# A norm's scale taken from half a row: the first feed-forward of a decoder layer

## The chip, the cores and the metric

The kernel runs on one core of one Trainium2 chip. The metric is the device time of one execution in microseconds, as the median of several runs. The engines are TensorE (PE, matrix products and transposes), VectorE (DVE), ScalarE (ACT), GpSimd (POOL) and SyncE (SP), whose queue issues nearly all DMAs.

## The reference

One layer on 256 tokens of width 2048, all in float32: a SwiGLU feed-forward of inner width 5632 (half of it added to the residual), a mixer, a cross-attention, a second such feed-forward and a last norm. The change touches the first feed-forward:

```python
def rmsnorm(x, g):
    xf = x.astype(jnp.float32)
    y = xf * lax.rsqrt(jnp.mean(xf * xf, axis=-1, keepdims=True) + EPS)
    return (y * g.astype(jnp.float32)).astype(x.dtype)

def swiglu(x, w_gate, w_up, w_down):
    return (jax.nn.silu(x @ w_gate) * (x @ w_up)) @ w_down

h = h + 0.5 * swiglu(rmsnorm(h, g_ffn1[l]), w1_gate[l], w1_up[l], w1_down[l])
```

## The kernel before

Every product is a sum of three in a reduced format: a float32 matrix is split into a rounded high half and the low half that is left (`split`: ACT casts the high half, DVE subtracts it for the low one), and high x high, low x high and high x low are accumulated. So every weight tile `f1gw` of 128 x 2048 costs ACT one cast (`f1gwh`) and DVE one subtraction (`f1gwl`).

The gate and up products of the first feed-forward run as eleven *units*, each of eight *chunks* along the inner dimension; a chunk is one weight tile of 1 MB against one *pair*, the two 128-column blocks of the 256 tokens' rows turned so that the inner dimension lies on the partitions. A chunk of kind N or C is 24 products of 128 x 512 on PE. Kind S multiplies 2 x 2 blocks by a seven-product scheme, 21 products; it needs sums of weight blocks (`f1gt`, and their halves `f1gth` and `f1gtl`) and sums of the pair's blocks (`n1f`, with high and low halves `n1fh` and `n1fl`). From the third unit on the chunks are S and C in turn.

The first unit (unit 0) doesn't wait for the norm. It multiplies the unnormalized rows, loaded already turned from `xT` (`n0r`, halves `n0h` and `n0l`) and scaled by the gain alone, and takes in the row's factor at the gating. Meanwhile the norm is made: four blocks of 512 columns of `h` are loaded, ACT squares and sums each for both token blocks (`square_into`, tile `junk`, sums in `parts`), `rstd_of` makes the factor (DVE reduces to `ss` and scales to `ms`, POOL raises to the power -1/2, `rs`), and `normalized(j)` has ACT scale two pairs' worth of rows at a time (`n1s`). PE then turns them by four transposes per pair (tile `n`), ACT applies the gain (`n1r`), and the halves are split. Units 1 to 10 read these pairs, eight of them, through `have(n1, i)`. The first serves unit 1's chunk 0.

`prep1(i)` is called once the load of chunk i of unit 0 is written, and with 8 + i beside chunk i of unit 1. It says at which chunk a block is loaded, squared and normalized. What it normalizes is turned by a generator, `work`, which is advanced after every sixth product, so its steps come at set places in PE's order. PE's order is the order in which the code issues. The other engines' orders are set by the scheduler of the framework, and all engines take their instructions in that order.

At a unit's end `late` combines the seven sums (`seven_late`, with DVE), and `gated` applies SiLU (ACT) and multiplies (DVE, line 699 without a factor, line 701 with one):

```python
nc.scalar.activation(sg[1], sg[0], AF.Silu, scale=1.0 if r is None else r[:, tb:tb + 1])
if r is None:
    nc.vector.tensor_tensor(sg[1], up, sg[1], ALU.mult)
else:
    nc.vector.scalar_tensor_tensor(
        out=sg[1], in0=up, scalar=r[:, tb:tb + 1], in1=sg[1], op0=ALU.mult, op1=ALU.mult
    )
```

Units 1 to 10 of the first feed-forward pass no factor. The second feed-forward does: its rows are scaled by the norm of their left half, and `rstd_left` makes what is left to the full norm. Tiles of the first feed-forward's gate units begin with `f1g`, those of the second with `f2g`. Banks of PE's accumulator are called `f1gP...`, `f1gQ...` and `f1gR`.

## Time and profile before

| | us |
|---|---|
| median of 3 runs | 2035.32 (2033.4 to 2035.91) |
| the profiled execution | 2033.63 |
| its span | 2031.9 |
| PE busy | 2015.5 (99%) |
| DVE busy | 1853.6 (91%) |
| ACT busy | 1313.2 (65%) |
| POOL busy | 34.4 (2%) |

The span runs from the first to the last recorded instruction; the profiled execution's time is 1.73 us longer. A row of a timeline gives the start and the length in microseconds, the engine, the line of the kernel, the operation, the tile written and the tiles read, and in brackets how long the engine had been idle and what released it. A row of waits gives a sum in microseconds, a count and the longest. Matmuls overlap, so their lengths say less than the distance of their starts.

### The profile page before, as it was taken

What the parts mean: (1) busy time and instruction counts of PE and PEld (TensorE: products, weight loads), DVE (VectorE), ACT (ScalarE), POOL (GpSimd) and SP (SyncE); (2) the same over time, 40 slices, a digit from 0 to 9 for tenths busy, and PEclk for the clock granted to TensorE, in tenths of its full rate; (3) what the DMA queues carried; (4) which work ended last, traced back from release to release, by engine and by line L of the source; (5) the groups of instructions that cost most, each with busy time, mean ns of one, the idle gap of its engine ahead of it and who ended that gap; (6) DMA issues with size and microseconds to landing.
All of it is one profiled execution on the core that took longest, in us unless ns stands there. A gap on an engine that the chain in (4) does not pass through costs nothing.

```text
span 2031.9 us, 24271 instructions
## 1 busy us (share of the span) xinstructions
PE 2015.5 (99%) x9203; PEld 1668.8 (82%) x9203; DVE 1853.6 (91%) x1994; ACT 1313.2 (65%) x1460; POOL 34.4 (2%) x57
## 2 busy tenths in 40 slices
PE   9999999999999999999999999999999999999998
PEld 7788888888888888888888888888888888888886
DVE  6999999999999978989879987899999999999998
ACT  7765566567665766755566666676656666676664
POOL 0000000000000010200000000000000000000000
PEclk9999999999999999999999999999999999999999
DMA  8666666666556575544675544556566656665563
GB/s 312 197 206 225 215 218 205 236 209 220 196 191 219 177 252 178 202 166 166 208 227 182 198 160 145 187 187 224 197 239 215 215 205 231 214 219 206 187 228 125
DMA packets 115333, 415.83 MB, mean 205 GB/s; under 512 B 61824, under 2 KB 63888, under 8 KB 68112
## 3 DMA queue, kind: packets, MB, share of 16 engines
q1 hardware_dynamic: 112768, 407.14, 57.6%
q0 software_dynamic: 2016, 6.30, 1.0%
q8 instruction: 72, 1.18, 0.2%
q10 hardware_dynamic: 432, 0.84, 0.1%
q14 instruction: 45, 0.37, 0.1%
HBM read 398.52 MB, written 2.10 MB: 197 GB/s over the span
## 4 chain that ended last, share of the span: by engine, by line
PE 85%; DVE 9%; issue 3%; ACT 2%; DMA 2%; SPq 0%; POOL 0%; POOLq 0%; DVEq 0%; ACTq 0%
PE f1gQ L428 12%; PE f2gQ L428 12%; PE f2dQ L428 6%; PE f1dQ L428 6%; PE f1gP L428 5%; PE f2gP L428 4%; PE xqQ L428 3%; PE f2dP L428 3%; PE f1dP L428 3%; PE woQ L428 2%; PE xoQ L428 2%; PE f2dR L428 2%; PE f1dR L428 2%; DVE f1gwl L148 2%; PE vQ L428 2%
## 5 line engine op out<-in xcount | busy, mean ns | idle before, releaser
L148 DVE TENSOR_TENSOR f1gwl<-f1gw,f1gwh 128x1536 fp32r<-128x1536 f32 (+2 forms) x94 | 181.6, 1934 | 24.5 <-ACT f1gwh L147 23.8
L147 ACT CAST f2gwh<-f2gw 128x1536 fp32r<-128x1536 f32 (+1 forms) x88 | 150.5, 1712 | 66.4 <-PE f2gQ L428 44.9
L148 DVE TENSOR_TENSOR f2gwl<-f2gw,f2gwh 128x1536 fp32r<-128x1536 f32 (+1 forms) x88 | 179.1, 2036 | 8.0 <-ACT f2gwh L147 8.0
L147 ACT CAST f1gwh<-f1gw 128x1536 fp32r<-128x1536 f32 (+2 forms) x94 | 153.1, 1629 | 45.0 <-PE f1gQ L428 19.3
L147 ACT CAST f1gth<-f1gt 128x1024 fp32r<-128x1024 f32 x76 | 79.9, 1051 | 103.1 <-DVE f1gt L337 68.7
L147 ACT CAST f2gth<-f2gt 128x1024 fp32r<-128x1024 f32 x82 | 85.4, 1050 | 64.2 <-DVE f2gt L341 34.0
L428 PE MATMUL f2gQ<-f2gwh,n4fh 128*128 128x512 f32 x317 | 123.8, 390 | 0.6 <-DVE f2gv L587 0.6
L428 PE MATMUL f2gQ<-f2gwh,n4fl 128*128 128x512 f32 x317 | 123.4, 389 | 0.0
L428 PE MATMUL f1gQ<-f1gwh,n1fl 128*128 128x512 f32 x286 | 111.4, 390 | 1.7 <-DVE n1fl L148 1.7
L428 PE MATMUL f1gQ<-f1gwh,n1fh 128*128 128x512 f32 x286 | 111.6, 390 | 0.0
L147 ACT CAST f2dwh<-f2dw 128x2048 fp32r<-128x2048 f32 (+1 forms) x44 | 77.4, 1758 | 47.5 <-PE f2dQ L428 39.5
L147 ACT CAST f1dwh<-f1dw 128x2048 fp32r<-128x2048 f32 (+1 forms) x44 | 77.3, 1757 | 43.7 <-PE f1dQ L428 42.7
L148 DVE TENSOR_TENSOR f1dwl<-f1dw,f1dwh 128x2048 fp32r<-128x2048 f32 (+1 forms) x44 | 92.0, 2092 | 12.0 <-ACT f1dwh L147 11.8
L148 DVE TENSOR_TENSOR f2dwl<-f2dw,f2dwh 128x2048 fp32r<-128x2048 f32 (+1 forms) x44 | 92.0, 2091 | 11.2 <-ACT f2dwh L147 11.1
L148 DVE TENSOR_TENSOR f2gtl<-f2gt,f2gth 128x1024 fp32r<-128x1024 f32 x82 | 99.5, 1218 | 1.0
L428 PE MATMUL f2gQ<-f2gwl,n4fh 128*128 128x512 f32 x317 | 96.7, 389 | 0.0
L148 DVE TENSOR_TENSOR f1gtl<-f1gt,f1gth 128x1024 fp32r<-128x1024 f32 x76 | 92.2, 1216 | 0.5
L428 PE MATMUL f1gQ<-f1gwl,n1fh 128*128 128x512 f32 x286 | 86.9, 389 | 0.0
L428 PEld LDWEIGHTS f2gQ<-f2gwh,n4fh 128*128 128x128 f32 x317 | 59.5, 188 | 13.8 <-DVE f2gv L587 1.6
L428 PEld LDWEIGHTS f2gQ<-f2gwh,n4fl 128*128 128x128 f32 x317 | 59.5, 188 | 12.2
L428 PEld LDWEIGHTS f2gQ<-f2gwl,n4fh 128*128 128x128 f32 x317 | 59.4, 188 | 12.3
L428 PE MATMUL f2gP<-f2gwh,n4fh 128*128 128x512 f32 x176 | 68.6, 390 | 0.0
(824 smaller groups left out, 6072.2 us busy)
## 6 DMA issues: line engine op xcount, KB each, us to landing
f2gw<-in_w_gu SPq DMA_DIRECT2D x88, 1024.0 KB, 4.9
f1gw<-in_w_gu SPq DMA_DIRECT2D x86, 1024.0 KB, 4.8
f1dw<-in_w_down SPq DMA_DIRECT2D x44, 1024.0 KB, 4.8
f2dw<-in_w_down SPq DMA_DIRECT2D x44, 1024.0 KB, 4.8
wow<-in_w_out SPq DMA_DIRECT2D x16, 1024.0 KB, 4.8
xqw<-in_w_xq SPq DMA_DIRECT2D x16, 1024.0 KB, 4.8
xow<-in_w_xo SPq DMA_DIRECT2D x16, 1024.0 KB, 4.8
qw<-in_w_in SPq DMA_DIRECT2D x8, 1024.0 KB, 4.8
```

The costliest lines, as they stand in the source:

```text
L147: nc.scalar.copy(hi, src)
L148: nc.vector.tensor_tensor(lo, src, hi.bitcast(F32), ALU.subtract)
L428: nc.tensor.matmul(self.banks[name], x, y, start=name not in self.begun, stop=self.left[name] == 0)
```

## The change

The factor for the normalized rows of the first feed-forward is made from the first two blocks of 512 columns, once these are squared (chunk 4), with `rstd_of(parts1[:, :, :2], 2, 1024)`. The normalizing of the four blocks is moved one chunk ahead (from 6, 8, 10, 12 to 5, 7, 9, 11). The full factor, which unit 0's gating needs, is made one chunk later, and beside it `rstd_left` makes the full norm's factor divided by the first one, which the gating of units 1 to 10 now takes.

```diff
     rs1 = []
+    est1, left1 = [], []
...
         for j in {4:(0,1),5:(2,3)}.get(i, ()):
             for tb in range(TB):
                 square_into(parts1[:, tb, j:j + 1], h[:, tb, j * 512:(j + 1) * 512], 512)
-        if i == 5:
+        if i == 4:
+            est1.append(rstd_of(parts1[:, :, :2], 2, 1024))
+        if i == 6:
             rs1.append(rstd_of(parts1, NG, D))
-        for j in {6:(0,),8:(1,),10:(2,),12:(3,)}.get(i, ()):
+            left1.append(rstd_left(parts1, est1[0]))
+        for j in {5:(0,),7:(1,),9:(2,),11:(3,)}.get(i, ()):
             normalized(j)
...
-                r[:, tb], h[:, tb, j * 512:(j + 1) * 512], AF.Copy, scale=rs1[0][:, tb:tb + 1]
+                r[:, tb], h[:, tb, j * 512:(j + 1) * 512], AF.Copy, scale=est1[0][:, tb:tb + 1]
...
     ffn(
-        "f1", lambda i: have(n1, i), lambda: None, w1_gu, w1_down, on2,
+        "f1", lambda i: have(n1, i), lambda: left1[0], w1_gu, w1_down, on2,
```

`rstd_left`, which was there before, adds four small operations on DVE and one on POOL:

```python
def rstd_left(parts, est):
    ss = tiny.tile([P, TB], F32, tag="ss", name=nm("ss"))
    nc.vector.tensor_reduce(out=ss, in_=parts, axis=AX.X, op=ALU.add)
    ms = tiny.tile([P, TB], F32, tag="ms", name=nm("ms"))
    nc.vector.tensor_scalar(ms, ss, 1.0 / D, EPS, op0=ALU.mult, op1=ALU.add)
    nc.vector.tensor_tensor(ms, ms, est, ALU.mult)
    nc.vector.tensor_tensor(ms, ms, est, ALU.mult)
    rs = tiny.tile([P, TB], F32, tag="rs", name=nm("rs"), bufs=8)
    nc.gpsimd.tensor_tensor(rs, ms, mhalf, ALU.pow)
    return rs
```

The change moves instructions on every engine. On ACT, around chunk 5 of unit 0 (its weights are `f1gwh_323` before and `f1gwh_329` now; `n0h_270` is the pair of chunk 5, `junk` the squares, `n1s` the scaled rows), there stood before:

```order
L147 CAST f1gwh_277<-f1gw_276 128x2048
L137 ACTIVATE junk_292,parts_117<-h 128x512
L141 ACTIVATE n0h_270<-n0r_282,sm 128x256 x2
L137 ACTIVATE junk_330,parts_117<-h 128x512
L137 ACTIVATE junk_332,parts_117<-h 128x512
L137 ACTIVATE junk_334,parts_117<-h 128x512
L147 CAST f1gwh_323<-f1gw_322 128x2048
L137 ACTIVATE junk_336,parts_117<-h 128x512
L141 ACTIVATE n0h_368<-n0r_328,sm 128x256 x2
L147 CAST f1gwh_375<-f1gw_374 128x2048
L917 ACTIVATE n1s_382<-h,rs_342 128x512 x2
```

And now:

```order
L147 CAST f1gwh_277<-f1gw_276 128x2048
L137 ACTIVATE junk_292,parts_117<-h 128x512
L141 ACTIVATE n0h_270<-n0r_282,sm 128x256 x2
L921 ACTIVATE n1s_344<-h,rs_298 128x512
L137 ACTIVATE junk_336,parts_117<-h 128x512
L137 ACTIVATE junk_338,parts_117<-h 128x512
L137 ACTIVATE junk_340,parts_117<-h 128x512
L147 CAST f1gwh_329<-f1gw_328 128x2048
L137 ACTIVATE junk_342,parts_117<-h 128x512
L921 ACTIVATE n1s_344<-h,rs_298 128x512
L141 ACTIVATE n0h_397<-n0r_334,sm 128x256 x2
```

The two scalings of the first rows moved from behind chunk 6's cast to both sides of chunk 5's cast and of the right half's squares.

On PE, at the end of chunk 4 (`f1gwl_278`), the next chunk's products followed before:

```order
L428 MATMUL f1gR_169<-f1gwl_278,n0h_270 128x512 x2
L428 MATMUL f1gQ_17_167<-f1gwl_278,n0h_270 128x512 x2
L428 MATMUL f1gP_16_166<-f1gwh_323,n0h_270 128x512
L428 MATMUL f1gP_16_166<-f1gwh_323,n0l_271 128x512
L428 MATMUL f1gP_16_166<-f1gwh_323,n0h_270 128x512
```

And now:

```order
L428 MATMUL f1gR_169<-f1gwl_278,n0h_270 128x512 x2
L428 MATMUL f1gQ_17_167<-f1gwl_278,n0h_270 128x512 x2
L248 MATMUL n_52_371<-ident,n1s_344 128x128 x4
L428 MATMUL f1gP_16_166<-f1gwh_329,n0h_270 128x512
L428 MATMUL f1gP_16_166<-f1gwh_329,n0l_271 128x512
```

The first pair's four transposes moved from the head of chunk 6 to the head of chunk 5.

On DVE, at the end of a later unit (`f1gv` and `f1u` hold the up halves, `f1gp` and `f1gz` the gated ones), there stood before:

```order
L148 TENSOR_TENSOR f1gtl_1526<-f1gt_1515,f1gth_1525 128x1024
L699 TENSOR_TENSOR f1gp_286_1505<-f1gv_1506,f1gp_286_1505 128x512
L699 TENSOR_TENSOR f1gz_1507<-f1u_1553,f1gz_1507 128x512
L148 TENSOR_TENSOR f1gwl_1569<-f1gw_1567,f1gwh_1568 128x2048
L337 TENSOR_TENSOR f1gt_1608<-f1gw_1604 128x1024
```

And now:

```order
L148 TENSOR_TENSOR f1gtl_1540<-f1gt_1529,f1gth_1539 128x1024
L701 SCALAR_TENSOR_TENSOR f1gp_292_1519<-f1gv_1520,rs_423,f1gp_292_1519 128x512
L701 SCALAR_TENSOR_TENSOR f1gz_1521<-f1u_1567,rs_423,f1gz_1521 128x512
L148 TENSOR_TENSOR f1gwl_1583<-f1gw_1581,f1gwh_1582 128x2048
L337 TENSOR_TENSOR f1gt_1622<-f1gw_1618 128x1024
```

Nothing moved there; the two products took a factor.

## The prediction

> **What bounds the kernel now.** I read the page first, then the table of what TensorE (PE) waits for, then the timelines of all engines over the first 120 us, where the change lies, and at last the chain of waits through the first feed-forward.

> ```profile
> span 2031.9 us, 24271 instructions
> ...
> PE 2015.5 (99%) x9203; PEld 1668.8 (82%) x9203; DVE 1853.6 (91%) x1994; ACT 1313.2 (65%) x1460; POOL 34.4 (2%) x57
> ...
> PE f1gQ L428 <- DVE n1fl L148: 1.7, 1, 1.7
> ...
> PE f1gQ L428 <- DVE f1gtl L148: 1.1, 4, 0.6
> ```

> PE is busy for all but 16.4 us of the span, start and tail included, so a change elsewhere wins or loses only through PE's few waits. The first feed-forward has two kinds, both for VectorE (DVE): one long wait for `n1fl`, the low half of a normalized pair, and short ones for `f1gtl`, the low half of the summed weights. On PE's timeline (start, length, what, and in brackets the idle time before):

> ```profile
> 34.97 0.39 PE L428 MATMUL f1gP<-f1gwh,n0h 128*128 128x512 f32 x1
> ...
> 40.41 0.60 PE L248 MATMUL n<-ident,n1s 128*128 128x128 f32 x4
> 40.77 0.48 PE L428 MATMUL f1gP<-f1gwh,n0h 128*128 128x512 f32 x1
> ...
> 65.80 0.48 PE L428 MATMUL f1gQ<-f1gwh,n1fh 128*128 128x512 f32 x1
> 67.96 0.50 PE L428 MATMUL f1gQ<-f1gwh,n1fl 128*128 128x512 f32 x1 [1.69 <-DVE n1fl L148]
> ...
> 112.86 0.62 PE L428 MATMUL f1gQ<-f1gtl,n1fh 128*128 128x512 f32 x2
> 114.07 0.73 PE L428 MATMUL f1gQ<-f1gtl,n1fh 128*128 128x512 f32 x2 [0.59 <-DVE f1gtl L148]
> ```

> Chunk 5 (counted from 0) of the first unit starts at 34.97 and, 24 matmuls later, the first four transposes of the normalized rows at 40.41: 5.44 us, 0.227 each. From 65.80 to 67.96 PE issued one matmul, so 1.93 us were lost, 2.0 with the slow restart. From 112.86 to 114.07 it issued two: 0.76 lost, 0.9 with the restart.

> **The change, part by part.**

> *The scale comes earlier.* The factor for `n1s` is now made from two squares per row, not four. DVE, POOL and ScalarE (ACT) around its making before:

> ```profile
> 27.80 2.29 DVE L148 TENSOR_TENSOR f1gwl<-f1gw,f1gwh 128x2048 fp32r<-128x2048 f32 x1 [2.88 <-ACT f1gwh L147]
> ...
> 33.62 2.29 DVE L148 TENSOR_TENSOR f1gwl<-f1gw,f1gwh 128x2048 fp32r<-128x2048 f32 x1 [2.73 <-ACT f1gwh L147]
> 35.83 0.15 DVE L126 TENSOR_REDUCE ss<-parts 128x2 f32<-128x8 f32 x1
> ...
> 36.54 0.89 POOL L132 TENSOR_TENSOR rs<-ms,mhalf 128x2 f32<-128x2 f32 x1 [33.19 <-DVE ms L130]
> ...
> 28.29 0.90 ACT L141 ACTIVATE n0h<-n0r,sm 128x256 fp32r<-128x256 f32 x2
> 29.09 0.62 ACT L137 ACTIVATE junk<-h 128x512 f32<-128x512 f32 x1
> ...
> 31.68 1.91 ACT L147 CAST f1gwh<-f1gw 128x2048 fp32r<-128x2048 f32 x1 [0.65 <-DMA f1gw<-in_w_gu]
> 33.49 0.62 ACT L137 ACTIVATE junk<-h 128x512 f32<-128x512 f32 x1
> ...
> 37.47 1.34 ACT L917 ACTIVATE n1s<-h,rs 128x512 f32<-128x512 f32 x2 [0.62 <-POOL rs L132]
> ...
> 39.51 0.71 ACT L917 ACTIVATE n1s<-h,rs 128x512 f32<-128x512 f32 x1
> ```

> From the end of the weight split ahead of it (33.62 + 2.29 = 35.91) to `n1s` at 37.47 the chain reduce, mean, power, scale takes 1.56 us. In the new order it stands behind the split of chunk 4, which ends at 30.09, so the first `n1s` can run at 31.65, 5.8 us earlier. But on ACT that first `n1s` now stands right behind `n0h` (which ends at 29.19), ahead of three squares of the right half and of the cast of chunk 5's weights. ACT stands from 29.2 to 31.65 and then works off: `n1s` 0.62, three squares at 0.62 each (34.13), the cast with a step of 1.81 (31.68 to 33.49; so 35.94), the last square (36.56), the second `n1s` of 0.71 (37.27). The four transposes need both `n1s`, and they now stand on PE ahead of chunk 5, which PE reaches at 34.97. The first is issued, the second waits until 37.3: **2.2 us of new PE wait**. The weights' cast alone would have held PE to 36.0, 1.0 us; nothing held it there before. Bounds: 0, if the factor is ready when ACT comes to it, and 3.4, if the chain takes 1.2 us longer. I take 2.2, since every duration in it is a row of this very place.

> That ACT does not let the squares pass is read from 31.68: ACT idled 0.65 for a DMA with a square behind it that waited for nothing new. [...]

> *The normalized pairs come a chunk earlier.* Same transposes, casts and subtractions. The pair that PE waited for at 67.96 is then ready some 9 us ahead of its use (its last subtraction follows the split of unit 1's first chunk by seven short operations on DVE). **Minus 2.0 us.**

> *What DVE then is late with.* Between 61 and 114 us DVE has a single pause of 0.31 us, so what is late at 114 is decided by DVE's own account up to there. Its pauses:

> ```profile
> 42.29 0.43 DVE L226 TENSOR_TENSOR n1f<-n1r 128x256 f32<-128x256 f32 x1 [2.17 <-ACT n1r L266]
> ...
> 44.09 2.29 DVE L148 TENSOR_TENSOR f1gwl<-f1gw,f1gwh 128x2048 fp32r<-128x2048 f32 x1 [0.51 <-ACT f1gwh L147]
> ...
> 59.34 1.76 DVE L148 TENSOR_TENSOR f1gwl<-f1gw,f1gwh 128x1536 fp32r<-128x1536 f32 x1 [0.75 <-ACT f1gwh L147]
> ...
> 102.65 0.69 DVE L699 TENSOR_TENSOR f1gz<-f1u,f1gz 128x512 f32<-128x512 f32 x1 [0.31 <-ACT f1gz L695]
> ...
> 120.47 2.29 DVE L148 TENSOR_TENSOR f1gwl<-f1gw,f1gwh 128x2048 fp32r<-128x2048 f32 x1 [1.06 <-ACT f1gwh L147]
> ...
> L862 DVE TENSOR_TENSOR ms<-ms,rs x3: 152/160/160, 707.3 to 1341.0; 128x2 f32<-128x2 f32 x3
> ```

> Added: chunk 5's split starts with the end of its cast at 35.97, not 33.62 (+2.35); six tiny operations for the second and third factor, two of 0.16 each from the last row and four like them, overlapping, +0.5; two new waits for casts that PE's lateness holds back, about 0.5 and 1.0 (from stepping ACT and DVE through the new order by hand with these durations); and 0.12 for the gating of unit 1 (next part). Used up: the pauses of 2.17, 0.51, 0.75 and 0.31, filled by pairs that come earlier (-3.74). Net: DVE reaches the `f1gtl` of 114 about **0.7 us later**. PE alone, at +2.2 - 2.0 - 0.9, would be 0.7 early there; DVE ends last, so the place counts +0.7. Bounds -0.7 (PE's account) and +2.0 (a third of the pauses unfilled).

> *The gating takes a factor.* In the ten units after the first, SiLU gets a scale per row and the product becomes a three-operand one. Both forms are in this trace, since the second feed-forward gates so already:

> ```profile
> L699 DVE TENSOR_TENSOR f1gz<-f1u,f1gz x10: 679/681/692, 102.6 to 473.6; 128x512 f32<-128x512 f32 x10
> ...
> L701 DVE SCALAR_TENSOR_TENSOR f2gz<-f2u,rs,f2gz x11: 739/743/752, 1385.5 to 1798.5; 128x512 f32<-128x512 f32 x11
> ...
> L695 ACT ACTIVATE f2gz<-f2gz,rs x11: 715/719/727, 1384.8 to 1795.6; 128x512 f32<-128x512 f32 x11
> ...
> L695 ACT ACTIVATE f1gz<-f1gz x10: 622/629/632, 102.0 to 472.9; 128x512 f32<-128x512 f32 x10
> ```

> DVE pays 743 - 681 = 62 ns and ACT 719 - 629 = 90 ns for each of two per unit. ACT's 0.18 a unit is covered: ACT is 65% busy, and in the unit shown next its SiLU had ended 0.9 us before the product that reads it. DVE's 0.124 is not, by the chain of waits (start, length, what):

> ```profile
> 136.58 4.08 PE f1gQ L428 x18
> ...
> 425.46 4.08 PE f1gQ L428 x18
> ...
> 226.45 0.68 DVE f1gz L699
> ...
> 236.60 1.23 DVE f1gtl L148
> ...
> 237.87 0.72 PE f1gQ L428 x2
> ...
> 1420.24 4.08 PE f2gQ L428 x18
> ...
> 1461.04 4.08 PE f2gQ L428 x18
> ```

> The same eighteen matmuls come back seven times between 136.58 and 425.46, every 41.27 us; in the second feed-forward every 40.80. The missing 0.47 is one wait per unit, for an `f1gtl` that stands on DVE behind the gating product without a pause. So seven units pay 0.124 each: **+0.87 us**. Bounds 0 and, with ACT's part too, 7 x 0.31 = 2.1.

> *Nothing else.* POOL gets two more powers of 0.9 us and is 2% busy. One load of `xT` moves behind one weight load on SP's queue, and is due only at chunk 7.

> **Sum:** +0.7 through 114 us, +0.87 after it: +1.6 us, 2033.5 for the span and 2035.2 for the profiled execution, which took 2033.63 (1.73 around the span). That execution lies 1.7 under the median of 2035.32, so by the median **2036.9 us**. Less than 0.2% (4.1 us) can't be told from no change in this kernel, whose three times spread over 2.5.

> **The rivals.**
> 1. The new wait doesn't come about or stays under 0.5 us: then -2.0, at most -0.9 at 114, and +0.87: -2.0, 2033.3. For it: ACT had 0.65 us of idle time there anyway. Against: the power on POOL alone is 0.89.
> 2. Faster: as 1, and the seven waits vanish as well, as the second feed-forward shows that units with this gating can run at 40.80: -2.0 - 0.9 - 7 x 0.47 = -6.2, 2029.1. Against: DVE's rows in those units keep their order, and the second feed-forward has another.
> 3. Slower: DVE's pauses are not filled. They were waits for ACT, and ACT is what becomes late; then the +2.35, +0.5, +1.5 and +0.12 stand without the -3.74: +4.5 at 114 and +5.3 in all, 2040.6. It decides from a pause of over 2 us left on DVE between 38 and 60 us.
> 4. Slower: PE's clock drops in the new wait. The 1.69 us at 66 left it whole:

> ```profile
> 60.00:80.00 20.00, 18.32 (x90) 14.93 (x89) 19.97 (x27) 16.50 (x25) 0.00 (x0) 1.00 0.57 192
> ```

> The last but two is the granted clock, 1.00. A wait of 2.2 is longer than any in the stage, and one chunk at half pace costs 5.44 more: +7.0, 2042.3. [...]

> **How the numbers follow.** The forecast has 0.65, rival 1 0.21, rival 2 0.04, rival 3 0.07, rival 4 0.03. Forecast and rival 1 lie within 0.2%, so same 0.86, faster 0.04, slower 0.10. The range runs from rival 1 (2033.3, less 0.5 for the spread) to the forecast with its upper bounds (+2.0 and +2.1: 2039.4).

> **What would show it.** Right: ACT idle about 2.4 us before `n1s` at 29 us; PE idle about 2 us before the transposes at 35; no wait for `n1fl`; an unchanged or longer wait near 114; spacing of the eighteen matmuls 41.39. Wrong: no PE wait at 35; a spacing of 41.27 or 40.80; a granted clock under 1; DVE pauses of 2 us between 38 and 60.

## The result and the profile after

| | before | changed |
|---|---|---|
| median of 22 runs each, us | 2033.91 (2032.66 to 2035.91) | 2038.37 (2035.48 to 2040.2) |
| ratio, 95% interval | | 1.0019 (1.0013 to 1.0025) |
| profiled execution, us | 2033.63 | 2038.31 |

The changed kernel is slower by 0.13 to 0.25%, 4.46 us by the medians. The forecast was 2036.9, 1.6 us more than before, with 2032.8 to 2039.4 as its range. The profile's head and TensorE's (PE) waits of the changed kernel (sum, count, longest):

```profile
span 2036.6 us, 24278 instructions
...
PE 2018.2 (99%) x9203; PEld 1670.2 (82%) x9203; DVE 1855.7 (91%) x2000; ACT 1315.2 (65%) x1460; POOL 35.7 (2%) x59
...
PE f1gQ L428 <- DVE f1gtl L148: 3.0, 9, 1.0
PE n L248 <- ACT n1s L921: 2.0, 1, 2.0
PE f2gQ L428 <- DVE f2gv L587: 1.4, 3, 0.7
```

The wait for `n1fl` is gone. A new one for `n1s` stands in its place, the one for `f1gtl` went from 1.1 to 3.0 us, and one in the second feed-forward, whose code did not change, went from 0.6 to 1.4.

The new wait, on POOL, ACT and PE (start, length, what; in brackets the idle time before):

```profile
30.04 0.89 POOL L132 TENSOR_TENSOR rs<-ms,mhalf 128x2 f32<-128x2 f32 x1 [26.70 <-DVE ms L130]
...
30.96 0.73 ACT L921 ACTIVATE n1s<-h,rs 128x512 f32<-128x512 f32 x1 [2.45 <-POOL rs L132]
...
33.44 1.88 ACT L147 CAST f1gwh<-f1gw 128x2048 fp32r<-128x2048 f32 x1
...
35.85 0.71 ACT L921 ACTIVATE n1s<-h,rs 128x512 f32<-128x512 f32 x1
...
34.37 0.27 PE L248 MATMUL n<-ident,n1s 128*128 128x128 f32 x1
36.61 0.55 PE L248 MATMUL n<-ident,n1s 128*128 128x128 f32 x3 [1.97 <-ACT n1s L921]
36.91 0.48 PE L428 MATMUL f1gP<-f1gwh,n0h 128*128 128x512 f32 x1
...
37.48 0.63 PE L428 MATMUL f1gP<-f1gwh,n0h 128*128 128x512 f32 x1
...
38.76 0.63 PE L428 MATMUL f1gQ<-f1gwh,n0l 128*128 128x512 f32 x1
39.19 1.06 PE L248 MATMUL n<-ident,n1s 128*128 128x128 f32 x4
...
40.88 0.40 PE L428 MATMUL f1gR<-f1gwh,n0h 128*128 128x512 f32 x1
41.11 0.39 PE L428 MATMUL f1gR<-f1gwh,n0l 128*128 128x512 f32 x1
```

ACT stands 2.45 us for the factor, and PE, which issues the first of four transposes at 34.37, the next at 36.61. Then something new: the products of chunk 5 are 0.43 us apart from 37.48 to 39.19 ((39.19 - 37.48) / 4), not 0.23 as again from 40.88 on. One-microsecond windows of the same stretch (the number behind the length is PE's busy time; the last three are the granted clock of PE, the DMA share and GB/s):

```profile
37.00:38.00 1.00, 1.00 (x6) 0.80 (x5) 1.00 (x3) 1.00 (x4) 0.00 (x0) 0.71 0.00 0
38.00:39.00 1.00, 1.00 (x4) 0.80 (x3) 1.00 (x4) 1.00 (x2) 0.00 (x0) 0.50 0.24 57
39.00:40.00 1.00, 1.00 (x6) 0.81 (x4) 0.90 (x8) 1.00 (x2) 0.20 (x1) 0.50 0.79 254
40.00:41.00 1.00, 1.00 (x5) 0.83 (x4) 0.61 (x3) 1.00 (x3) 1.00 (x2) 0.58 1.07 451
```

The granted clock is 0.50 from 37.4 to 40.8 us. PE counts as busy meanwhile (1.00 of the microsecond from 38 to 39, at 0.50), so no table of waits shows this loss.

The wait for `f1gtl` has moved too. The end of unit 1 on DVE, before and then after:

```profile
96.39 0.68 DVE L341 TENSOR_TENSOR f1gt<-f1gt,f1gw 128x512 f32<-128x512 f32 x1
96.99 0.68 DVE L586 TENSOR_TENSOR f1u<-f1gQ,f1gz 128x512 f32<-128x512 f32 x1
97.59 0.68 DVE L587 TENSOR_TENSOR f1gv<-f1gQ,f1gv 128x512 f32<-128x512 f32 x1
98.19 1.21 DVE L148 TENSOR_TENSOR f1gtl<-f1gt,f1gth 128x1024 fp32r<-128x1024 f32 x1
```

```profile
99.64 0.69 DVE L341 TENSOR_TENSOR f1gt<-f1gt,f1gw 128x512 f32<-128x512 f32 x1
100.23 0.69 DVE L588 TENSOR_TENSOR f1gv<-f1gQ,f1gv 128x512 f32<-128x512 f32 x1
100.83 0.69 DVE L589 TENSOR_TENSOR f1gz<-f1gQ,f1gz 128x512 f32<-128x512 f32 x1
101.43 0.75 DVE L701 SCALAR_TENSOR_TENSOR f1gp<-f1gv,rs,f1gp 128x512 f32<-128x512 f32 x1
102.09 1.23 DVE L148 TENSOR_TENSOR f1gtl<-f1gt,f1gth 128x1024 fp32r<-128x1024 f32 x1
...
103.37 0.50 PE L428 MATMUL f1gQ<-f1gtl,n1fh 128*128 128x512 f32 x1 [0.96 <-DVE f1gtl L148]
```

The sum `f1gt` is done 3.25 us later, and the scheduler now has three operations between it and `f1gtl` instead of two; `f1gtl` starts 3.9 us later, and PE waits for it at 103 instead of 114.

In each unit after that, PE waits for `f1gtl` a little longer than before; the first and the last of the seven:

```profile
157.33 0.73 PE L428 MATMUL f1gQ<-f1gtl,n1fh 128*128 128x512 f32 x2 [0.28 <-DVE f1gtl L148]
...
405.51 0.72 PE L428 MATMUL f1gQ<-f1gtl,n1fh 128*128 128x512 f32 x2 [0.27 <-DVE f1gtl L148]
```

Six units lie between: (405.51 - 157.33) / 6 = 41.36 us a unit, where it was 41.27.

### The profile page after: what moved, and what is told of

Read it like the earlier page. It is cut to its first block, busy times and chain, and to the rows that moved or that the text cites. A ratio compares the mean times of both kernels' runs of the same rounds, so it can differ in the third digit from the quotient of the medians.

```text
span 2036.6 us, 24278 instructions
## 1 busy us (share of the span) xinstructions
PE 2018.2 (99%) x9203; PEld 1670.2 (82%) x9203; DVE 1855.7 (91%) x2000; ACT 1315.2 (65%) x1460; POOL 35.7 (2%) x59
## 4 chain that ended last, share of the span: by engine, by line
PE 79%; DVE 12%; issue 5%; ACT 2%; DMA 1%; POOL 0%; SPq 0%; POOLq 0%; DVEq 0%; ACTq 0%
PE f2gQ L428 13%; PE f1gQ L428 7%; PE f2dQ L428 6%; PE f1dQ L428 6%; PE f2gP L428 4%; PE xqQ L428 3%; DVE f1gwl L148 3%; PE f2dP L428 3%; PE f1gP L428 3%; PE f1dP L428 3%; PE woQ L428 2%; PE xoQ L428 2%; PE f2dR L428 2%; PE f1dR L428 2%; PE vQ L428 2%
## 5 line engine op out<-in xcount | busy, mean ns | idle before, releaser
L148 DVE TENSOR_TENSOR f1gwl<-f1gw,f1gwh 128x1536 fp32r<-128x1536 f32 (+2 forms) x94 | 182.0, 1937 | 28.0 <-ACT f1gwh L147 27.0
L147 ACT CAST f2gwh<-f2gw 128x1536 fp32r<-128x1536 f32 (+1 forms) x88 | 150.4, 1711 | 61.6 <-PE f2gQ L428 42.9
L148 DVE TENSOR_TENSOR f2gwl<-f2gw,f2gwh 128x1536 fp32r<-128x1536 f32 (+1 forms) x88 | 179.5, 2040 | 9.6 <-ACT f2gwh L147 9.1
L147 ACT CAST f1gwh<-f1gw 128x1536 fp32r<-128x1536 f32 (+2 forms) x94 | 153.1, 1629 | 44.0 <-PE f1gQ L428 18.5
L147 ACT CAST f1gth<-f1gt 128x1024 fp32r<-128x1024 f32 x76 | 79.9, 1052 | 106.1 <-DVE f1gt L337 72.0
L147 ACT CAST f2gth<-f2gt 128x1024 fp32r<-128x1024 f32 x82 | 85.9, 1050 | 67.8 <-DVE f2gt L341 38.5
L428 PE MATMUL f2gQ<-f2gwh,n4fh 128*128 128x512 f32 x317 | 124.1, 392 | 1.5 <-DVE f2gv L587 1.4
L428 PE MATMUL f2gQ<-f2gwh,n4fl 128*128 128x512 f32 x317 | 123.4, 389 | 0.0
L428 PE MATMUL f1gQ<-f1gwh,n1fh 128*128 128x512 f32 x286 | 111.8, 391 | 0.0
L428 PE MATMUL f1gQ<-f1gwh,n1fl 128*128 128x512 f32 x286 | 111.3, 389 | 0.0
L147 ACT CAST f2dwh<-f2dw 128x2048 fp32r<-128x2048 f32 (+1 forms) x44 | 77.4, 1759 | 47.4 <-PE f2dQ L428 39.5
L147 ACT CAST f1dwh<-f1dw 128x2048 fp32r<-128x2048 f32 (+1 forms) x44 | 77.3, 1756 | 42.4 <-PE f1dQ L428 41.2
L148 DVE TENSOR_TENSOR f1dwl<-f1dw,f1dwh 128x2048 fp32r<-128x2048 f32 (+1 forms) x44 | 92.3, 2098 | 12.1 <-ACT f1dwh L147 11.9
L148 DVE TENSOR_TENSOR f2dwl<-f2dw,f2dwh 128x2048 fp32r<-128x2048 f32 (+1 forms) x44 | 92.3, 2097 | 11.2 <-ACT f2dwh L147 10.8
L148 DVE TENSOR_TENSOR f2gtl<-f2gt,f2gth 128x1024 fp32r<-128x1024 f32 x82 | 99.9, 1222 | 1.0
L428 PE MATMUL f2gQ<-f2gwl,n4fh 128*128 128x512 f32 x317 | 96.7, 389 | 0.0
L148 DVE TENSOR_TENSOR f1gtl<-f1gt,f1gth 128x1024 fp32r<-128x1024 f32 x76 | 92.7, 1221 | 0.7 <-ACT f1gth L147 0.3
L428 PE MATMUL f1gQ<-f1gwl,n1fh 128*128 128x512 f32 x286 | 86.9, 389 | 0.0
L428 PEld LDWEIGHTS f2gQ<-f2gwh,n4fh 128*128 128x128 f32 x317 | 59.5, 188 | 15.7 <-DVE f2gv L587 3.5
L428 PEld LDWEIGHTS f2gQ<-f2gwl,n4fh 128*128 128x128 f32 x317 | 59.4, 188 | 12.3
L428 PEld LDWEIGHTS f2gQ<-f2gwh,n4fl 128*128 128x128 f32 x317 | 59.5, 188 | 12.0
L428 PE MATMUL f2gP<-f2gwh,n4fh 128*128 128x512 f32 x176 | 68.6, 390 | 0.0
```

What stands on the lines that cost most here:

```text
L147: nc.scalar.copy(hi, src)
L148: nc.vector.tensor_tensor(lo, src, hi.bitcast(F32), ALU.subtract)
L428: nc.tensor.matmul(self.banks[name], x, y, start=name not in self.begun, stop=self.left[name] == 0)
```

## The experiments

All kernels issue the same products in the same stages (one has ten more), so one comparison serves for all: how much later PE starts the same product than in the profile of before, and how much of that is added between two landmarks (us of the profile before; a plus is a loss). The start of the table is 18.5 us, since the executions already lie 0.2 to 1.1 us ahead of the profile of before there, ahead of any change. A set of four transposes that stood behind 58.0 before stands ahead of it in every kernel with earlier pairs. That puts about 0.5 us into the first column and takes it out of the second: rest_early, which has no new wait, adds +0.49 up to 58.0.

| added between | 18.5 and 58.0 | 58.0 and 71.8 | 71.8 and 114.6 | 114.6 and 403.5 | 403.5 and 538 | 538 and 1716 |
|---|---|---|---|---|---|---|
| changed | +4.36 | -2.55 | +0.66 | +0.71 | +0.19 | +1.87 |
| changed, again | +4.36 | -2.55 | +0.68 | +0.74 | +0.16 | 0.00 |
| gate_only | 0.00 | -0.03 | +0.15 | +0.82 | +0.20 | +0.62 |
| move_only | +2.80 | -2.55 | +0.48 | -0.02 | -0.12 | +1.23 |
| move_only, again | +5.11 | -2.56 | +0.51 | -0.19 | -0.13 | +1.39 |
| wait_filled | +2.75 | -2.56 | +0.65 | +0.79 | +0.22 | +0.08 |
| wait_filled, again | +3.83 | -2.55 | +0.65 | +0.72 | +0.17 | +2.95 |
| rest_early | +0.49 | -2.55 | +1.41 | -3.03 | -0.14 | +0.52 |
| rest_early, again | +0.59 | -2.55 | +1.40 | -3.08 | -0.15 | +0.22 |
| first_back | +0.59 | -2.56 | +2.91 | -1.54 | +0.18 | +0.15 |
| first_back, again | +0.64 | -2.55 | +2.91 | -1.32 | +0.15 | +1.60 |

**gate_only: the gating's factor alone.** The kernel before, with a column of ones as the factor.

```diff
-        "f1", lambda i: have(n1, i), lambda: None, w1_gu, w1_down, on2,
+        "f1", lambda i: have(n1, i), lambda: ones, w1_gu, w1_down, on2,
```

> The kernel before, with the gating of units 1 to 10 given a factor per row that is 1.0 everywhere (a column of ones), and nothing else: the same order on every engine, the three-operand product and the SiLU with a scale in place of the plain ones. If the gating costs what the changed kernel's profile shows (seven waits per unit grown from 0.43 to 0.55 us): +0.8 us, at most +1.2. If the gating is the main cost of the change (the rival): +3 us or more.

2035.05 us against 2034.27 of the kernel before beside it, ratio 1.0004 (0.9995 to 1.0013). The median is up 0.8 us, but the interval alone doesn't tell it from nothing. The table does: the seven units after 114.6 add +0.82, 0.12 each, unit 1 adds 0.15, and the stretch ahead nothing. The changed kernel adds +0.71 and +0.74 there. This term is shown.

**move_only: the earlier scale alone.** The changed kernel without the left factor, which leaves its rows at the scale of the left half.

```diff
-        "f1", lambda i: have(n1, i), lambda: left1[0], w1_gu, w1_down, on2,
+        "f1", lambda i: have(n1, i), lambda: None, w1_gu, w1_down, on2,
```

> The changed kernel without the factor at the gating of units 1 to 10 (the left factor is left out of the computation there). If the early move costs what the ledger of the changed kernel shows (2.0 wait, 1.4 of half pace, less 2.0 at the old wait, and a wait of 1.7 at 103 us for one of 0.9 at 114): +2 to +3 us against the kernel before, and the units' spacing back at 41.27. If the gating is the main cost: within 0.5 us of the kernel before.

2036.62 us, ratio 1.0012 (1.0003 to 1.0021). The units add nothing (-0.02), so what the gating costs and what the move costs are two separate things. Its profile has the new wait, but behind it the clock stays whole:

```profile
PE n L248 <- ACT n1s L921: 2.0, 1, 2.0
...
38.00:39.00 1.00, 1.00 (x8) 0.83 (x8) 1.00 (x4) 1.00 (x2) 0.00 (x0) 1.00 0.48 66
```

Up to 58 us it adds 2.80 where the changed kernel adds 4.36: the half pace is worth 1.56 us, close to half of its 3.4 us.

**wait_filled: ten products in the new wait.** They go to a bank that nobody reads; every other engine's order is the changed kernel's.

```diff
+                if j == 0 and q == 0:
+                    fill_ = bank("fill")
+                    x = n0[4].base[0]
+                    for _ in range(10):
+                        nc.tensor.matmul(
+                            fill_, x[:, 0, :], x.rearrange("p k t -> p (k t)"), start=True, stop=True
+                        )
```

> The changed kernel with ten more products of 128x512 on TensorE, into a bank that nobody reads, ahead of the first transposes, where TensorE waits 2.0 us for the scaled rows; the other engines' orders are unchanged. If the idle time itself is what brings the slow stretch (0.43 us between products from 37.5 to 40.9 us): no idle, no slow stretch, 0.227 us between products after the transposes, and the time 1.4 us under the changed kernel. If the stretch has another cause (ScalarE's and VectorE's traffic, or chance): same time as the changed kernel, or 0.1 to 0.3 more.

2038.22 us, ratio 1.002 (1.0012 to 1.0029): as slow as the changed kernel. In the profile the fill did what it was for:

```profile
34.38 2.43 PE L932 MATMUL fill<-n0h 128*128 128x512 f32 x10
36.65 0.60 PE L248 MATMUL n<-ident,n1s 128*128 128x128 f32 x4
```

The clock stays whole behind it (1.00 in every microsecond from 34 to 2029 us), and up to 58 us it adds 2.75, like move_only. But that profiled execution took 2035.12 us, the shortest of this kernel's eleven. What the others lose is not in it, so its time doesn't show that filling the wait pays.

**rest_early: the other three blocks alone.** The kernel before, full factor, block 0 where it was, the others a chunk earlier.

```diff
-        for j in {6:(0,),8:(1,),10:(2,),12:(3,)}.get(i, ()):
+        for j in {6:(0,),7:(1,),9:(2,),11:(3,)}.get(i, ()):
```

> The kernel before with the full norm's factor kept, the first block of 512 columns normalized at chunk 6 as it was, and the other three one chunk earlier (7, 9, 11). No wait for the factor, no factor at the gating. If the gain of the change lies in the earlier pairs alone: the wait of 2.0 us for the third pair's low half is gone, and the time is 1 to 2 us under the kernel before. If earlier pairs only crowd VectorE and the wait comes back elsewhere (the rival; the changed kernel had 1.7 us at 103): within 0.5 us of the kernel before.

2031.99 us against 2034.27 of the kernel before, ratio 0.9988 (0.9979 to 0.9997): faster by 0.03 to 0.21%, and faster than the changed kernel. The `n1fl` wait goes without the new one. DVE pays part of it back at unit 1's end, but the seven later waits for `f1gtl` are gone as well, where DVE's order in the units is another (that this order is the cause was not tried by itself); eighteen products of the chain come back every (421.33 - 135.51) / 7 = 40.83 us:

```profile
100.75 0.50 PE L428 MATMUL f1gQ<-f1gtl,n1fh 128*128 128x512 f32 x1 [1.85 <-DVE f1gtl L148]
...
135.51 4.08 PE f1gQ L428 x18
...
421.33 4.08 PE f1gQ L428 x18
```

**Three kernels once more.** The same kernels, each with one more profile, for what the slower executions lose.

> The changed kernel again, for one more profile. If the half-pace stretch behind the new 2 us TensorE wait at 35 us is a fixed part of the change, the matmuls at 37.5 to 41 us are again 0.43 us apart and the kernel ends near 2038.3 us. If it comes by chance, they are 0.23 us apart in some executions, and the time is then nearer 2036.5 us. The waits for f1gtl near 103 us (1.1 us) and of 0.55 us per unit should be there either way.

> The changed kernel with ten matmuls in the new wait, once more. Its median of 2038.2 us lay 3 us above its profiled execution (2035.1 us). If the slower executions lose their time at one place, this profile shows it: theory A, in the stage from the second feed-forward's start to its end (454.6 us in the first profile, up to 456.5 us in others); theory B, at a half-pace stretch somewhere in the first 60 us; theory C, spread over all stages.

> The kernel before with the second halves' normalization one chunk earlier, once more: 2030 to 2033 us. If the stage of the second feed-forward varies by itself from one execution to another, it lies between 454.6 and 456.5 us here too; if that variation belongs to the changed kernel alone, it stays within 0.3 us of the 455.3 us of the first profile.

2036.25, 2038.28 and 2029.59 us. The changed kernel again had a wait of 1.95 us and the half pace behind it, so the half pace alone is not what sets 2036.25 apart from 2038.31: it adds the same +4.36, and the whole difference is in the last column, the second feed-forward. There wait_filled, in its second profile, loses 2.95 us. Of the waits in that profile, ACT's for a weight load between 1600 and 1640 us and, over the whole execution, PE's in this stage:

```profile
ACT f2gwh L147 <- DMA f2gw<-in_w_gu: 4.5, 1, 4.5
...
PE f2gP L428 <- DVE f2gwl L148: 1.5, 2, 1.3
PE f2gQ L428 <- DVE f2gv L587: 1.4, 2, 0.9
```

ACT waited 4.5 us for one weight load there (2.3 in the same place before). The code is the same in all of these kernels at that place; the column spreads over 0 to 2.95 us.

There is a second such place, far ahead of it. ACT's cast of chunk 4's weights waits for its load, 1.35 to 1.44 us in eight of the fourteen profiles and 2.22 to 2.56 in the other six, the kernels without block 0 at chunk 5 among both. In move_only's two profiles (the second is reported below):

```profile
25.31 1.92 ACT L147 CAST f1gwh<-f1gw 128x2048 fp32r<-128x2048 f32 x1 [1.40 <-DMA f1gw<-in_w_gu]
...
26.25 1.91 ACT L147 CAST f1gwh<-f1gw 128x2048 fp32r<-128x2048 f32 x1 [2.42 <-DMA f1gw<-in_w_gu]
```

With block 0 at chunk 6 the late load costs nothing up to 58 us (rest_early +0.49 with it, +0.59 without; first_back +0.64 and +0.59). With block 0 at chunk 5 the factor, the cast and `n1s` stand behind it, and PE waits for it: wait_filled adds +3.83 with it and +2.75 without, since ten products no longer fill the wait, and move_only's wait at 35 us is 2.81 with it and 1.99 without.

**first_back: the changed kernel with block 0 back at chunk 6.**

```diff
-        for j in {5:(0,),7:(1,),9:(2,),11:(3,)}.get(i, ()):
+        for j in {6:(0,),7:(1,),9:(2,),11:(3,)}.get(i, ()):
```

> The changed kernel, with the second half of row block 0 normalized at chunk 6 as in the kernel before and the others at 7, 9 and 11; the factor of chunks from 5 on stays that of the left half. If the new wait at 35 us and the f1gtl wait moved to 103 us are what the change costs beside the gating, the wait at 35 us goes and the time is the kernel before's less the n1fl wait (2.0 us) and plus the gating (0.8 us): 2032 to 2034 us. If the changed factor itself were the cost, it stays near 2037 us.

2032.21 us beside 2035.09 of the kernel before, ratio 0.9987 (0.9978 to 0.9996). So with one number back the loss is gone: what the change loses hangs on block 0 at chunk 5, and the median shows no cost of the changed factor. By the table its units still lose about 1.5 us to rest_early's (-1.54 against -3.03), where the gating alone cost gate_only +0.82. The seven waits for `f1gtl` are gone here too. The half pace came back at another place, behind another wait of its size:

```profile
101.15 0.50 PE L428 MATMUL f1gQ<-f1gtl,n1fh 128*128 128x512 f32 x1 [1.98 <-DVE f1gtl L148]
...
103.00:104.00 1.00, 1.00 (x4) 0.81 (x3) 1.00 (x1) 0.28 (x1) 0.00 (x0) 0.50 0.46 92
```

Against rest_early's +1.41 it adds +2.91 there, 1.50 more for 0.13 us more of wait; unit 1's gating may be 0.15 of it, as in gate_only. In rest_early the clock stayed at 1.00 behind its 1.85 us, in both profiles.

**What it takes to lose the clock.** Two more squares on ACT in the changed kernel, to make the new wait longer, and one more profile of move_only and of first_back.

```diff
+        if i == 5:
+            for tb in range(TB):
+                square_into(parts1[:, tb, 3:4], h[:, tb, 3 * 512:4 * 512], 512)
```

> The changed kernel with two more squares on ScalarE ahead of the second n1s, so that TensorE waits about 1.4 us longer at 35 us: 3.4 us, not 2.0. Theory A, the granted clock halves for about 3.5 us after an idle time from about 2 us on: the row of 38 to 39 us shows 0.50, the matmuls behind the transposes are 0.43 us apart. Theory B, the two stretches seen were chance and idle time has no part in them: spacing 0.23 and clock 1.00 as likely as not. The operations behind the transposes also change places on ScalarE and VectorE, so its whole time, about 2036 to 2041 us, is no evidence.

> The same kernel once more. Theory A: again 0.50 for the granted clock at 38 to 39 us, in both of two profiles. Theory B: 0.50 in one or in none.

> The changed kernel without the left factor at the gating, once more. Its first profile had the wait of 1.99 us at 35 us with the granted clock at 1.00 behind it, where two profiles of the changed kernel had 0.50 behind waits of 1.95 and 1.97. If a wait of 2.0 us lies at the edge, either can come: with the half clock the time is 1.0 to 1.5 us above 2034.9 us, without it the same. The waits at 35 us (2.0) and 102 us (0.9) should be there again.

> The changed kernel with row block 0 back at chunk 6, once more. Its first profile had a wait of 1.98 us for f1gtl at 101 us and the granted clock at 0.50 behind it; the kernel before with the other blocks a chunk earlier had 1.85 us there, twice, at 1.00. If about 2 us is the edge, a wait again of 1.9 to 2.0 us may go either way: 2031 to 2034 us with the half clock, 2029.7 to 2031.5 us without.

2040.81, 2040.12, 2037.55 and 2034.28 us. All four have the half pace. wait_longer's wait came out at 4.35 and 4.15 us, more than the 3.4 expected (chunk 4's load was late in both), and in its first profile the half pace is twice as long as elsewhere, from 36.6 to 43.4 us. The wait there and two of the windows:

```profile
PE n L248 <- ACT n1s L924: 4.3, 1, 4.3
...
36.00:37.00 1.00, 0.00 (x0) 0.00 (x0) 0.77 (x1) 1.00 (x4) 0.00 (x0) 0.80 0.06 25
...
41.00:42.00 1.00, 1.00 (x4) 0.60 (x4) 0.71 (x1) 1.00 (x4) 0.00 (x0) 0.50 1.06 451
```

And move_only's second profile, whose wait came out at 2.81 us and not at the 2.0 expected, with the late load above:

```profile
37.67 0.81 PE L248 MATMUL n<-ident,n1s 128*128 128x128 f32 x3 [2.81 <-ACT n1s L921]
...
39.00:40.00 1.00, 1.00 (x4) 0.71 (x4) 1.00 (x4) 1.00 (x2) 0.00 (x0) 0.50 0.58 66
```

In order of the wait, over all profiles and all waits above 1.3 us: 1.67, 1.69, 1.85 and 1.85 us left the clock whole; 1.95, 1.95, 1.97 and 1.98 lost it, 1.99 (move_only's first) did not; 2.81, 4.15 and 4.35 lost it. That idle time has no part in it is ruled out, but the length alone doesn't decide.

```profile
34.01:37.42 3.41, 1.44 (x9) 1.00 (x8) 2.07 (x1) 3.41 (x7) 0.00 (x0) 1.00 0.43 180
37.42:40.83 3.41, 3.41 (x11) 2.75 (x10) 2.92 (x14) 3.41 (x6) 1.03 (x2) 0.50 0.55 195
...
31.64:35.05 3.41, 3.11 (x15) 2.29 (x13) 0.00 (x0) 3.41 (x8) 0.00 (x0) 1.00 1.01 421
35.05:38.46 3.41, 1.72 (x9) 1.47 (x10) 2.97 (x3) 3.41 (x9) 0.00 (x0) 1.00 0.14 60
38.46:41.88 3.42, 3.42 (x18) 2.86 (x17) 2.91 (x12) 3.32 (x5) 1.35 (x2) 1.00 0.85 304
```

The changed kernel's wait lies in one window, which is idle for 3.41 - 1.44 = 1.97 us, and the next runs at half pace. The 1.99 us of move_only fall on two, 0.30 and 1.69, and no half pace follows. So it is throughout: in the fourteen profiles, from the clock's first entry on, every window with 1.95 us or more of idle time on PE was followed by one at half pace, and none with 1.89 us or less (idle time is counted from the ends of products, which these profiles model, so the bound between the two is not sharp).

## Why the prediction came out as it did

The forecast's median lies 1.5 us under the measured one, and its place was right: within 0.2%, on the slower side. The two changes lie further apart, +1.6 forecast and +4.46 measured: the forecast started from a median of three runs, 2035.32, and 22 runs gave 2033.91. That the time still lies in the range is in part luck. The range's upper end was made of more for DVE and for the gating, which both came out as forecast; what filled it was the clock and other losses that the sum doesn't have. The part of the change that was forecast is +1.81 by the changed kernel's row up to 538 us, less the 1.56 of the half pace, where the sum said +1.6. By its steps:

- **The new wait on ACT and PE: right.** Predicted: ACT stands for the factor from 29.2 to 31.65 (2.45), PE waits 2.2. Measured: 2.45, and 1.97 (2.24 from one transpose to the next). So also its reason: ACT let none of the squares pass in these 2.45 us; the first starts at 31.59, behind `n1s`.
- **The `n1fl` wait: right.** Gone in every kernel with earlier pairs: -2.55 between 58.0 and 71.8, about -2.1 without the transposes that moved across 58.0, where -2.0 was predicted. The slow restart in that sum is 0.11 us: in the trace of before, the product behind the one at 67.96 starts 0.34 us after it and not 0.23. Its row there:

```profile
68.30 0.39 PE L428 MATMUL f1gQ<-f1gwl,n1fh 128*128 128x512 f32 x1
```

  Together with the new wait, and at whole clock, that is +0.25 (move_only: +2.80 - 2.55) where +0.2 was predicted.
- **DVE's account through 114 us: right in size, wrong in place.** Predicted +0.7; by the table from 18.5 to 114.6 it is +0.73 in move_only and +0.84 in wait_filled, at whole clock. But the sign that I named, an unchanged or longer wait near 114, did not come. I carried the order at unit 1's end over from before, but the scheduler had put `f1gtl` behind one more operation there, and PE's wait stands at 103. That the sizes agree is in part luck, and move_only's figure doesn't hold the 0.12 for the gating of unit 1.
- **The gating: right.** Predicted 7 x 0.124 = 0.87 with a spacing of 41.39; measured +0.71 to +0.82, spacing 41.36. ACT's share stayed hidden.
- **Rivals 1 to 3 did not come.** Of rival 3: between 38 and 60 us the longest DVE pause is this one, not 2 us.

```profile
50.29 2.29 DVE L148 TENSOR_TENSOR f1gwl<-f1gw,f1gwh 128x2048 fp32r<-128x2048 f32 x1 [0.65 <-ACT f1gwh L147]
```

  Rival 2's vanished waits came in rest_early, which does not have the factor at the gating, and in first_back, which has it.
- **Rival 4 came, at another price, and that is the step that failed.** It had a chance of 0.03 and a price of 5.44 us, one chunk at half pace. The clock was halved in both profiles of the changed kernel, and it costs 1.56 us, since the half pace lasts 3.4 us and not for a chunk's 24 products. That 2.2 us of idle time would be safe was my estimate, and no run shows it; the trace had a wait of 1.69 with the clock whole, and that one lay across two windows, with 0.64 and 1.05 us in them, and said nothing of a longer one. The premise at the head of the prediction, that a change wins or loses only through PE's waits, fails here too: PE counts as busy at half pace, 1.00 of the microsecond from 38 to 39. In these runs 1.95 us of idle time were enough when they lay in one window of 3.41.

The mean granted clock of every execution bears this out in part. A half-pace stretch takes 0.0008 off it, and none of the seven profiles with one reads 0.999. (The clock also drops to 0.50 at the very end, for the last 5.73 us of the span before, 5.80 in the changed kernel and 6.4 in rest_early, so a 0.998 proves no stretch.) Of the changed kernel's 22 runs, seven read 0.999, with a median of 2036.00; the fifteen others have 2039.00. The former lie 2.1 us above the median before of 2033.91, near the forecast's +1.6.

**What stays open.** Eight of eleven runs of wait_filled read 0.999 and still have a median of 2038.97, so the half pace can't be the whole of it. The profiles show two other losses that come in some executions and not in others. The late load of chunk 4's weights costs move_only 0.8 and wait_filled 1.1 us, and nothing where block 0 stands at chunk 6: this part belongs to the change, though neither profile of the changed kernel itself has it. The second feed-forward adds 0.15 to 1.60 in the kernels without block 0 at chunk 5 and 0.00 to 2.95 in those with it; the largest came with a late weight load. Why loads come late, and whether the change makes that likelier in the second feed-forward, no run here decides. The spread of the runs doesn't either: some 5 us with block 0 at chunk 5, 5.5 in first_back, which has it at chunk 6, and some 3 in the kernel before. How often each loss falls on an execution is not known, so the measured 4.46 us are not divided among them.

## What to carry to other kernels

A move that makes one wait go and another of the same length come is not neutral: the new one must be priced with the clock it may cost, and a wait just under 2 us (1.95 here) was already long enough for that when it fell in one window of the clock. Moving work earlier pays for the parts that have slack and costs for the one that doesn't: three of the four moves here are worth 2.3 us (ratio 0.9988), and the fourth takes that and more. A chain without slack also passes on what is late ahead of it, here a weight load of some executions. Where a scheduler orders an engine, the order at each place that PE waits for has to be read again after the change; here DVE's new order went with a wait that moved by 11 us and, in rest_early and first_back, with the end of seven.

## What the hardware showed unexpectedly

The half pace lasts 3.41 us in each of the six profiles where it lasts one window, one of them behind a wait of 4.15, and 6.83, two windows, behind a wait of 4.35 that left 2.24 us of idle time in one window and 2.11 in the next. It begins up to 0.9 us after the work has resumed, or while the engine still waits (at 36.6, in a wait that ends at 38.7), since it begins at a border of the windows. These borders lie at another place in each profile: the clock's first entry comes between 3.96 and 7.10 us (5.48 before, 6.70 in the changed kernel). So, by these numbers, the same wait of 2.0 us can cost 1.56 us more in one execution (1.97 in the changed kernel) and nothing more in another (1.99 in move_only), and a wait that once left the clock whole is no proof that it always will.
